# PSUM banks dealt out anew before the last blocks of the attention pass: two for value products and two for projections in place of one and three

## The chip, the cores and the metric

One NeuronCore of a Trainium2 chip runs the whole kernel. The metric is device time in microseconds (us), lower is better. Five engines work from queues of their own: TensorE (PE in the profile; its weight loads are PEld), VectorE (DVE), ScalarE (ACT), GpSimd (POOL) and SyncE (SP, which issues transfers). TensorE writes only to PSUM, which this kernel divides into eight banks; one bank holds a tile of 128 partitions by 512 fp32 values. ACT and DVE read the result out of a bank ("evict" it), and only then may TensorE start the next tile in the same bank.

## The reference

One encoder layer over x of 4096 tokens by 1024 features, with two groups of heads side by side, fp32 throughout. Only what matters here is kept:

```python
hn = rms_norm(x, norm_w)
proj = hn @ w_in                      # 1024 x 3856, cut into the parts below
qk_a, v_a, o_a, z_a, g_a, q_b, k_b, v_b, z_b = split(proj)
# group A: mLSTM, 4 heads x 128, both directions, short convolution on q and k
qk_a = silu(centred_depthwise_conv(qk_a, conv_w, conv_b))
h = sigmoid(o_a) * (mlstm(q_a, k_a, v_a, gates) + backwards mlstm)
y_a = head_norm(h) * silu(z_a)
# group B: attention in blocks of 128 queries over 384 keys, |i-j| <= 128,
# 8 query heads, 2 key/value heads of 64, a bias by distance, a sink per head
p = exp(scores + bias - m);  denom = sum(p) + exp(sink - m)
y_b = (p @ v_b) / denom * silu(z_b)
return rms_norm(x + concat(y_a, y_b) @ w_out, final_norm_w)
```

## The kernel before

The kernel runs four stages. **Pass 1** normalises x, keeps its transposed high and low parts in DRAM (`xT_d`), and computes the attention of group B. **Pass 2** goes backwards over the tokens and computes values, keys and queries of group A, their convolution and the chunks' outer products. **Pass 3** runs the mLSTM forwards. The **tail** does the gate of group B, the output projection and the last norm. An fp32 product is made of three reduced-precision products (low by high, high by low, high by high), so a projection of 1024 features is 8 x 3 = 24 matmuls into one bank. TensorE's order is written by hand (`manual_schedule` for PE); the order of ACT, DVE and POOL is laid out ahead by a planner, which goes by its own estimate of times and by priority, earlier program lines first. Each engine runs its queue strictly in that order.

**PSUM.** `c.psum(nb)` closes the pool of banks in use and opens a new one; `c.ps(tag, ...)` takes a tile of the pool that is open, from the banks of its tag. With `reuse_waits="tile"`, a tile of a new pool waits only for the tiles of the old one that lay in the same bank. Banks are dealt to tags in the order in which the tags are first used. The pool that is opened at the start, `{"pj": 3, "a": 2, "b": 2, "c": 1}`, therefore lies so: pj in banks 0 to 2, c in 3, a in 4 and 5, b in 6 and 7. It serves pass 1 and pass 2; the next call is at L1016, at the head of pass 3 (`{"pj": 2, "n": 2, "c": 1, "y": 1}`, pj in banks 0 and 1), the last at the head of the tail (`{"pj": 8}`).

**Pass 1** works on slots: slot `sl` is one block of 128 queries (n = sl // 2) for one of the two key heads. Its tiles are

- `sp`, tag a: scores of one of four heads (L359, two matmuls), evicted by DVE at L362;
- `tp`, tag b: four transposes for one of three key blocks (L387), evicted by ACT at L389 and DVE at L390;
- `op`, tag c: the value product, two matmuls for each of the three key blocks (L401), evicted by ACT at L413 and then by DVE at L414 (`AB`);
- tag pj: the projections, `qp` (L524, 24 matmuls; evicted at L534 by ACT, L538 by DVE), `kp` (L460; L471 and L472 by ACT, L476 and L477 by DVE), `vp` (L492 and L493; L498 by ACT, L499 by DVE) and `v2p` (L574; L579 by ACT).

A slot's pieces, written `p = [Sc(0), O(0), Sc(1), T(0), O(1), Sc(2), T(1), O(2), Sc(3), T(2)]`, take the scores of two slots ahead, the transposes of its own and the value product of the slot before. `interleave` spreads these pieces evenly over the matmuls of the projections. The main loop runs 13 rounds of four slots; after it the last twelve slots (52 to 63) are interleaved with the last projections, in this order: four `qp` of block 14, `kp` 15, `vp` 30 and 31, four `qp` of block 15, and `v2p` 31 to 28. At the seam, the first piece that runs is the scores of slot 54, and then three matmuls of the first `qp`, the value product of slot 51, four more of `qp`, and the scores of slot 54's second head. In the program before, the last tiles in their banks at that point are: `kp` 14 in bank 0, `vp` 29 in bank 1, `vp` 28 in bank 2, `op` of slot 50 in bank 3, the scores of slot 53 in 4 and 5.

**Pass 2** goes over eight blocks b = 7 to 0 of 512 tokens. For each block but the first it makes four value tiles `v2p` (L829, 24 matmuls each, evicted by ACT at L835), two at a time: three matmuls of the one, three of the other, through eight k. Then come the keys `up` m = 4 to 7 and the queries m = 0 and 1 (L856, 24 matmuls each, evicted by ACT at L860, after which ACT starts the convolution at L872), one after another. `last_two` then makes m = 2 and m = 3, again three matmuls of the one and three of the other (in block 7 each tile is in two parts, and only the second parts alternate). All of these are tag pj:

```python
vu = [vproj(4 * b + i) for i in pair]          # pairs (3, 2), (1, 0)
for k in range(KT):
    for u in vu[0][3 * k:3 * k + 3] + vu[1][3 * k:3 * k + 3]:
        u()
...
for k in range(KT):                            # last_two
    out += p2[-1][k] + p3[-1][k]
```

In between stand, in tags a and b, the transposes of the keys (`ktp`, L904) and the outer products (`kv`, L158 to L160, evicted by ACT at L934 and DVE at L935). Nothing in pass 2 uses tag c.

**Pass 3** begins with the projections `op` and `zp` of tokens 0 to 127 and `op` of the next (L1148, evicted from L1155 on by ACT).

Of the kernel before, what the change touches and what calls it, by code (L numbers as in the profile page):

```python
# [131 lines left out]
def interleave(fill, pieces):  # L132
    cum = np.cumsum([0.0] + [getattr(f, "cost", 1.0) for f in fill])
    done = 0
    for i, p in enumerate(pieces):
        while done < len(fill) and cum[done + 1] <= cum[-1] * i / len(pieces) + 1e-6:
            fill[done]()
            done += 1
        p()
    for f in fill[done:]:  # L140
        f()
# [26 lines left out]
def pass1(c):  # L168
    nc, tc, A = c.nc, c.tc, c.A
    NB = 16  # L170
    with ExitStack() as es:
# [437 lines left out]
        for b in range(NB - 3):  # L609
# [10 lines left out]
                f2.insert(p, u)  # L620
            interleave(f2, A2)
        c.x7 = XT
        pieces = []
        for sl in range(4 * (NB - 3), 4 * NB):
            pieces += slot(sl)
# [844 lines left out]
def body(nc, tc, A):  # L1470
    with ExitStack() as es:
        c = setup(nc, tc, A, es)
        c.w3, c.w4, c.XR = [], [], {}

        def next_weights(i):
            c.w3.append(wgroup(c, (1536, 2048, 2560)[i], f"w3_{i}"))

        c.next_weights = next_weights
        with tc.manual_schedule(engines={mybir.EngineType.PE}):
            pass1(c)  # L1480
            pass2(c)
            pass3(c)
            c.psum_es.close()
# [43 lines left out]
```

## Time and profile before

| | |
|---|---|
| Median of 3 runs | 2218.36 us (2217.43 to 2219.31) |
| The profiled execution | 2218.53 us, of which 2216.8 us span |
| Pass 1, to the last value projection | 0 to 608 us |
| of it the last twelve slots | 499 to 608 us |
| Pass 2 | 608 to 1192 us |
| Pass 3 and tail | 1192 to 2217 us |

In the rows shown further on, a group's row has the engine, line, operation and tiles (out<-in), the count, busy time and the idle time just before it with what ended it. A row of the waits has what waited, for what, the total in us, how often, and the longest. A row of the timeline has the start and the length in us, engine, line, operation, tiles and count, and in brackets the idle time before. The windows' rows have, for a stretch of time, its length, the busy time of each engine with its count of instructions, then TensorE's granted clock as a share of full speed (PEclk), the DMA engines' share and GB/s. A matmul of 512 columns lasts 0.39 us but the next starts some 0.23 us after it, so rows overlap by about 0.16 us.

### The profile page before, as it was taken

To read this page: it belongs to the slowest core of one execution; us is meant where nothing else is said; L and a number is where in the kernel's file an instruction comes from. 1 tells how busy PE (TensorE), PEld (TensorE's weight loads), DVE (VectorE), ACT (ScalarE), POOL (GpSimd) and SP (SyncE) were. 2 spreads that over 40 slices of the span, in tenths; PEclk is the share of its full clock that TensorE was granted. 3 is DMA by queue.
4 is the path that set the end of the run, shared out by engine and by line. 5 is a ranking of instruction groups with operands and counts; after the bars stand their busy time and mean duration, and the time that the engine had idled before them with its cause. 6 is when DMAs were issued, how large, how long until landed. Compare 5 with 4: busy or idle time off the path is not lost.

```text
span 2216.8 us, 35208 instructions
## 1 busy us (share of the span) xinstructions
PE 2165.7 (98%) x12226; PEld 1880.3 (85%) x12226; DVE 1407.0 (63%) x3090; ACT 1075.4 (49%) x2711; POOL 607.3 (27%) x1059
## 2 busy tenths in 40 slices
PE   7999999999999999999999999999999999999998
PEld 6899999998797888888887888888888888888886
DVE  5687777787865566556667555455554443877776
ACT  5788888887643343334445434444443321333323
POOL 2565665662121211121112111111111111112222
PEclk9999999999999999999999999999999999999999
DMA  7653555432233452344267976777785898667774
GB/s 235 184 158 114 170 142 125 156 109 76 86 95 114 158 163 80 116 158 154 80 196 217 302 226 209 240 239 229 215 251 176 306 355 290 183 185 185 190 193 140
DMA packets 249126, 398.98 MB, mean 180 GB/s; under 512 B 21971, under 2 KB 128467, under 8 KB 248948
## 3 DMA queue, kind: packets, MB, share of 16 engines
q1 hardware_dynamic: 220628, 303.57, 45.1%
q0 software_dynamic: 28176, 92.96, 13.1%
q8 instruction: 96, 1.57, 0.3%
q14 instruction: 82, 0.67, 0.1%
q10 hardware_dynamic: 144, 0.20, 0.0%
HBM read 275.99 MB, written 120.67 MB: 179 GB/s over the span
## 4 chain that ended last, share of the span: by engine, by line
PE 77%; DMA 9%; issue 5%; DVE 4%; ACT 3%; POOL 2%; SPq 1%; POOLq 0%; DVEq 0%; ACTq 0%
PE up L856 15%; PE op L1148 7%; PE zp L1148 7%; PE qp L524 7%; PE v2p L829 7%; DMA xr<-x 5%; PE op L401 4%; PE tp L387 3%; PE sp L359 3%; PE zbp L158 3%; PE zbp L160 3%; PE zbp L159 3%; PE num L1101 2%; PE num L1100 2%; PE o L1314 2%
## 5 line engine op out<-in xcount | busy, mean ns | idle before, releaser
L856 PE MATMUL up<-xb,w 128*128 128x512 f32 x1344 | 338.4, 396 | 0.0
L1314 PE MATMUL o<-wo,yo 128*128 128x512 f32 (+1 forms) x1356 | 312.3, 392 | 0.0
L1314 PEld LDWEIGHTS o<-wo,yo 128*128 128x128 f32 x1356 | 253.2, 188 | 59.2
L856 PEld LDWEIGHTS up<-xb,w 128*128 128x128 f32 x1344 | 243.7, 188 | 47.2
L874 DVE SCALAR_TENSOR_TENSOR qk<-U,cw,qk 128x512 f32<-128x512 f32 x256 | 190.1, 755 | 93.4 <-ACT qk L872 89.6
L524 PE MATMUL qp<-xT,wqb 128*128 128x256 f32 x1536 | 246.2, 291 | 0.0
L524 PEld LDWEIGHTS qp<-xT,wqb 128*128 128x128 f32 x1536 | 217.9, 193 | 9.8 <-issue 1.7
L1148 PE MATMUL op<-w,xs 128*128 128x512 f32 x720 | 203.9, 411 | 2.4 <-ACT E L1069 2.4
L1148 PE MATMUL zp<-w,xs 128*128 128x512 f32 x720 | 188.6, 402 | 2.4 <-DVE z L1157 2.4
L829 PE MATMUL v2p<-w,xb 128*128 128x512 f32 x672 | 157.8, 395 | 0.6 <-DMA xb<-xT_d 0.5
L1148 PEld LDWEIGHTS zp<-w,xs 128*128 128x128 f32 x720 | 131.2, 189 | 29.4 <-DVE z L1157 2.8
L829 PEld LDWEIGHTS v2p<-w,xb 128*128 128x128 f32 x672 | 126.0, 188 | 31.1 <-DMA xb<-xT_d 1.5
L1115 ACT ACTIVATE hs<-num,r 128x128 f32<-128x128 f32 x128 | 46.9, 367 | 216.4 <-DVE r L1112 173.3
L362 DVE CUSTOM_DVE_ANT_0 s<-sp,G 128x320 f32<-128x320 f32 (+1 forms) x256 | 122.8, 480 | 41.5 <-PE sp L359 38.5
L1148 PEld LDWEIGHTS op<-w,xs 128*128 128x128 f32 x720 | 127.8, 191 | 24.0 <-ACT E L1069 2.8
L371 ACT ACTIVATE s<-s,st 128x320 f32<-128x320 f32 (+1 forms) x256 | 139.8, 549 | 12.4 <-DVE st L369 12.0
L390 DVE TENSOR_TENSOR pt<-tp,pt 128x512 fp32r<-128x512 f32 x188 | 129.3, 688 | 25.3 <-ACT pt L389 24.2
L389 ACT CAST pt<-tp 128x512 fp32r<-128x512 f32 x188 | 109.9, 586 | 58.1 <-PE tp L387 54.9
L401 PE MATMUL op<-pt,v 128*128 128x512 f32 x376 | 121.5, 404 | 13.2 <-DVE ab L414 13.2
L359 PE MATMUL sp<-kk,q 128*128 128x320 f32 (+2 forms) x512 | 118.8, 313 | 0.0
L387 PE MATMUL tp<-ident,s 128*128 128x128 f32 x752 | 113.8, 274 | 0.2 <-DVE pt L390 0.2
L158 PE MATMUL zbp<-xc,w 128*128 128x512 f32 x256 | 101.5, 397 | 0.0
(273 smaller groups left out, 4443.3 us busy)
## 6 DMA issues: line engine op xcount, KB each, us to landing
xc<-xT_d SPq DMA_DIRECT2D x64, 512.0 KB, 8.0
xs<-xT_d SPq DMA_DIRECT2D x120, 256.0 KB, 6.4
xT_d<-xT POOLq DMA_DIRECT2D x104, 256.0 KB, 5.5
xb<-xT_d SPq DMA_DIRECT2D x48, 514.0 KB, 10.7
E<-m_d SPq DMA_DIRECT2D x64, 256.0 KB, 4.7
W<-w_d SPq DMA_DIRECT2D x64, 256.0 KB, 5.8
y<-y_d SPq DMA_DIRECT2D x32, 512.0 KB, 3.5
out<-xr POOLq DMA_DIRECT2D x31, 512.0 KB, 4.5
```

The source lines that it names most:

```text
L158: nc.tensor.matmul(out, wl, xh, start=first, stop=False)
L359: nc.tensor.matmul(sp[:, lo:hi], qt, kk[:, kv, z, col - 128 + lo:col - 128 + hi], start=(z == 0), stop=(z == 1))
L371: nc.scalar.activation(ps[g][:, kept(g)], ps[g][:, kept(g)], AF.Exp, bias=ng[:, g:g + 1], accum_out=rs[:, g:g + 1])
L387: nc.tensor.transpose(tp[:, g * 128:(g + 1) * 128], ps[g][:, j * 128:(j + 1) * 128], c.ident)
L390: nc.vector.tensor_sub(pt[:, 1, :], tp, f32(pt[:, 0, :]))
L401: nc.tensor.matmul(op, vt, pt[:, z, :], start=(i == 0 and z == 0), stop=(i == len(js) - 1 and z == 1))
L524: nc.tensor.matmul(qp, wq[k // 2][:, k % 2, w, m * 128:m * 128 + 128], x[k], start=(k == 0 and j == 0), stop=(k == KT - 1 and j == 2))
L829: nc.tensor.matmul(vp, a, wv[k // 2][:, k % 2, m, :], start=(k == 0 and j == 0), stop=(k == KT - 1 and j == 2))
L856: nc.tensor.matmul(up[:, 0:hi - lo], w[k // 2][:, k % 2, a, cs], x, start=(k == 0 and j == 0), stop=(k == KT - 1 and j == 2))
L874: nc.vector.scalar_tensor_tensor(acc, U[:, t:t + 512], cw[:, cm, t:t + 1], acc, ALU.mult, ALU.add)
L1148: nc.tensor.matmul(P[nm], XS[n](a, k), w[:, m, :], start=(k == 0 and j == 0), stop=(k == KT - 1 and j == 2))
L1314: nc.tensor.matmul(p, a[:, z, k, :], w[k // 2][:, k % 2, m, lo:hi], start=k == 0 and z == 1, stop=k == 3 and z == 0 and m == 0)
```

## The change

Before the last twelve slots, one call opens a new pool of banks:

```diff
             interleave(f2, A2)
         c.x7 = XT
+        c.psum({"pj": 2, "a": 2, "b": 2, "c": 2})
         pieces = []
         for sl in range(4 * (NB - 3), 4 * NB):
             pieces += slot(sl)
```

From there on tag c has two banks and tag pj two in place of three; a and b keep two each. No instruction is added or taken away, and TensorE's order stays. By the order of first use (scores, projection, value product, transposes) the new pool lies so: a in banks 0 and 1, pj in 2 and 3, c in 4 and 5, b in 6 and 7. The pool stays open until the call at L1016, so it serves the whole of pass 2 too.

## The prediction

> **What bounds the kernel now.** I read the page's head, then TensorE's waits from 470 to 612 us, the stage that the change names, and then the windows and the timeline of pass 2, because the new pool stays open there.
>
> ```profile
> span 2216.8 us, 35208 instructions
> PE 2165.7 (98%) x12226; PEld 1880.3 (85%) x12226; DVE 1407.0 (63%) x3090; ACT 1075.4 (49%) x2711; POOL 607.3 (27%) x1059
> ...
> PE op L401 <- DVE ab L414: 9.2, 7, 3.5
> ...
> 700.00:1190.00 490.00, 489.00 (x2327) 404.63 (x2327) 309.96 (x479) 202.94 (x370) 96.34 (x216) 1.00 0.42 134
> ```
>
> The reader is to see three things. TensorE is busy for 98% of the span, so the kernel is as long as TensorE's order plus its stalls. In the last slots the value product waits for its one bank, 9.2 us in 7 waits: that is what the change can win there. In pass 2 (last row) TensorE is busy 489 of 490 us: a stall made there lengthens the kernel by its own size.
>
> **Part one, the second bank of the value product.** The timeline of TensorE, and then of DVE:
>
> ```profile
> 498.92 0.50 PE L359 MATMUL sp<-kk,q 128*128 128x320 f32 x2
> 499.25 0.51 PE L524 MATMUL qp<-xT,wqb 128*128 128x256 f32 x3
> 503.28 0.89 PE L401 MATMUL op<-pt,v 128*128 128x512 f32 x2 [3.51 <-DVE ab L414]
> 504.83 0.73 PE L359 MATMUL sp<-kk,q 128*128 128x320 f32 x2
> ...
> 513.89 0.74 PE L401 MATMUL op<-pt,v 128*128 128x512 f32 x2 [0.61 <-DVE ab L414]
> ...
> 516.50 0.62 PE L401 MATMUL op<-pt,v 128*128 128x512 f32 x2
> ...
> 536.30 0.34 PE L492 MATMUL vp<-wkv,xT 128*128 128x288 f32 x1
> ...
> 565.17 0.60 PE L387 MATMUL tp<-ident,s 128*128 128x128 f32 x4
> ...
> 568.41 0.74 PE L401 MATMUL op<-pt,v 128*128 128x512 f32 x2 [1.65 <-DVE ab L414]
> ...
> 583.46 0.60 PE L387 MATMUL tp<-ident,s 128*128 128x128 f32 x4
> ...
> 585.32 0.73 PE L401 MATMUL op<-pt,v 128*128 128x512 f32 x2 [0.33 <-DVE ab L414]
> ...
> 600.56 0.74 PE L401 MATMUL op<-pt,v 128*128 128x512 f32 x2 [1.07 <-DVE ab L414]
> ```
>
> ```profile
> 502.55 0.68 DVE L414 TENSOR_TENSOR ab<-op,ab 64x512 f32<-64x512 f32 x1
> ...
> 503.95 0.29 DVE L499 TENSOR_TENSOR vg<-vp,vg 128x144 f32<-128x144 f32 x1
> ...
> 536.22 0.43 DVE L477 TENSOR_TENSOR kk<-kp,kk 64x256 fp32r<-64x256 f32 x1
> ...
> 564.19 0.69 DVE L390 TENSOR_TENSOR pt<-tp,pt 128x512 fp32r<-128x512 f32 x1
> ...
> 582.11 0.69 DVE L390 TENSOR_TENSOR pt<-tp,pt 128x512 fp32r<-128x512 f32 x1
> ```
>
> *The price of a wait.* L414 ends at 503.23 and the value product starts at 503.28: 0.05 us from eviction to start. Behind a stall the pair of matmuls takes 0.74 us, without one 0.62: 0.11 us more, rounded. So a stall costs the missing time plus 0.16 us.
>
> *The first stall (3.51 us) mostly stays.* In the new pool the value product of slot 51 gets bank 4, long free. But after slot 54's first score (498.92), three matmuls of the projection, that product and four matmuls more comes slot 54's second score, now in bank 1, where `vp` 29 lies, and L499 reads that until 504.24. TensorE would reach this score at about 500.6, stand until 504.29, and be there 0.5 us earlier than now (504.83). That is all: **0.5**.
>
> *The six others* are 9.2 - 3.5 = 5.7 us, with the restarts (6 x 0.11) 6.4. They vanish wholly if evictions move up with TensorE. *What is late next:* `vp` 31, with two projection banks, needs the bank of `kp` 15, which L477 leaves at 536.65; it starts at 536.30 now, so it loses 0.35 + 0.16 = 0.5. Upper end of the gain: 0.5 + 6.4 - 0.5 = **6.4**. Lower end: DVE keeps its present times. Then the transposes at 565.17 cannot start before 564.93 (L390 ends at 564.88), so of all that was won before only 0.24 is left; the stall at 568.41 gives 1.65 + 0.11; the transposes at 583.46 wait for L390's end at 582.80 and cut what is won to 0.6; the last two stalls give 0.33 + 1.07 + 0.22: **2.2**. DVE does have idle time, so part of its work moves up; neither end is nearer, and I take the middle, **4.3 us won**.
>
> **Part two, pass 2 with two projection banks in place of three.** One seam between blocks, block 6 to 5, TensorE and then ACT, which stands for the other five:
>
> ```profile
> 743.13 22.46 PE L829 MATMUL v2p<-w,xb 128*128 128x512 f32 x96
> 765.43 1.33 PE L856 MATMUL up<-xb,w 128*128 128x512 f32 x5
> ```
>
> ```profile
> 742.63 0.59 ACT L860 COPY U<-up 128x512 f32<-128x512 f32 x1
> 743.25 0.82 ACT L872 ACTIVATE qk<-U,cb,cw 128x512 f32<-128x512 f32 x1
> 743.97 0.57 ACT L860 COPY U<-up 128x512 f32<-128x512 f32 x1
> ...
> 753.78 0.59 ACT L835 COPY v<-v2p 128x512 f32<-128x512 f32 x1 [2.77 <-PE v2p L829]
> ...
> 764.93 0.59 ACT L835 COPY v<-v2p 128x512 f32<-128x512 f32 x1 [3.94 <-PE v2p L829]
> ```
>
> The 96 matmuls start 0.232 us apart ((765.43 - 743.13) / 96). Where tiles are made two at a time, both banks are full at the end, and with only two banks the next tile must wait for a copy out of PSUM that takes 0.59 us; the third bank hid this.
>
> - First value tile: wants to start at 743.13, its bank (m = 2) is free at 743.22: 0.09 + 0.16 = 0.25.
> - Its partner: 3 matmuls later, 743.83, now 744.08. Its bank (m = 3) is free only at 744.54, since ACT does the convolution's L872 between the two copies: 0.46 + 0.16 = 0.62.
> - First tile of the second pair: 743.13 + 48 x 0.232 = 754.27, bank free at 754.37: 0.10 + 0.16 = 0.26. Its partner has the same distance, but is already 0.26 late: nothing.
> - First key tile: 765.43, bank free at 765.52: 0.25.
>
> That is 0.87 at each of six such seams and 0.51 in each of seven blocks: 5.2 + 3.6 = 8.8. Nothing hides it, as TensorE has no idle time there. Block 7 to 6 is different:
>
> ```profile
> 660.12 1.11 PE L856 MATMUL up<-xT,w 128*128 128x256 f32 x8
> 667.51 8.59 PE L829 MATMUL v2p<-w,xb 128*128 128x512 f32 x36
> 676.57 14.56 PE L829 MATMUL v2p<-w,xb 128*128 128x512 f32 x60 [0.48 <-DMA xb<-xT_d]
> ```
>
> ```profile
> 660.59 0.36 ACT L860 COPY U<-up 128x258 f32<-128x258 f32 x1
> ...
> 667.65 0.70 ACT L860 COPY U<-up 128x256 f32<-128x256 f32 x2
> ```
>
> The second part of m = 3 starts with the third matmul from 660.12 on, at 660.36, and its bank is free at 660.95: 0.59 + 0.16 = 0.75. The first value tile, 667.51, waits for the first of two copies, until 668.0: 0.5 + 0.16 = 0.66, of which the wait for a transfer at 676.57 takes back up to 0.48. I take 1.2. Part two: **10.0 us lost**. Bounds: without the restarts (0.11 each, 28 of them) 7; and if another order of ACT sets an operation of L872's 0.82 us before one copy in each block, 4 more, 14.
>
> **Part three, the head of pass 3.** Its first tile lies in bank 0, now last used by m = 3, afterwards by `kv`:
>
> ```profile
> 1192.33 5.84 PE L1148 MATMUL op<-w,xb 128*128 128x512 f32 x24 [1.44 <-ACT U L860]
> ...
> 1204.40 5.87 PE L1148 MATMUL op<-w,xb 128*128 128x512 f32 x24 [0.67 <-ACT o L1155]
> ```
>
> The 1.44 go, but the third tile waits for ACT's L1155 in any case, 6 us after the first tile's end (1192.33 + 5.84 to 1204.40): the wait of 0.67 grows instead. I take **0**, at best 1.5 won.
>
> **Sum.** The profiled execution took 2218.53 us, 0.17 over the median of 2218.36. 2218.5 - 4.3 + 10.0 = **2224.2 us**, slower by 0.26%. Bounds of the sum: 7 - 6.4 - 1.5 = -0.9 to 14 - 2.2 = +11.8, so 2217.6 to 2230.3.
>
> **The rivals.**
>
> *A wash.* Evictions move up with TensorE, all of part one comes to 6.4: 2222.1 us, inside 0.2%. For it: DVE is busy 63% of the span, so it has room to follow. Against: two tiles of transposes stand within 0.3 and 0.7 us of their own evictions.
>
> *Not slower.* The planner, seeing other banks, puts L499 ahead of DVE's backlog, and the first stall goes too. The rows:
>
> ```profile
> 498.21 1.84 DVE L559 SCALAR_TENSOR_TENSOR w<-w2s,nw,w 128x512 fp32r<-128x512 f32 x1
> ...
> 500.42 0.28 ACT L498 COPY vg<-vp 128x144 f32<-128x144 f32 x1
> ...
> 503.20:506.80 3.60, 3.52 (x16) 3.38 (x16) 2.24 (x8) 1.54 (x6) 1.31 (x5) 0.57 0.28 100
> 514.40:518.00 3.60, 3.60 (x29) 3.47 (x29) 2.54 (x9) 3.18 (x12) 0.20 (x1) 1.00 0.38 135
> 558.60:562.00 3.40, 3.40 (x25) 3.22 (x26) 2.69 (x8) 2.04 (x6) 2.54 (x3) 1.00 0.08 30
> ```
>
> It decides where L499 ends before 500.6, for which L498 on ACT must come earlier too. Price: 3.5 - 0.5 = 3.0, and the slow clock behind that stall (0.57 for 3.6 us, 1.5 us lost). With 6.4 and 1.5 at the head of pass 3, 12.4 won against 10.0: 2216.1 us; with part two at its lower end 2213.
> Against: L498 needs the last matmul of `vp` 29, which stands beside the score at 498.92, and L559 has begun by then.
>
> *The wrong bank.* Slot 54's first score, not its second, gets `vp` 29's bank: TensorE stands from 498.9 to 504.3 ahead of the value product, which then starts at about 505.1 in place of 503.28. Instead of 0.5 won, 1.8 lost: 2226.5 us.
>
> *Many small stalls slow the clock.* If each of seven seams brought the 1.5 us of a slow clock, 10.5 more: 2234.7 us. Against: behind the stalls of 0.61 and 1.58 us the granted clock was 1.00 (last two rows); only the one of 3.51 was followed by 0.57. The Trainium skill, page "TensorE: Matmul & The Clock Gate", section "A second HAM failure mode: psum-queue depth-cycling", tells of a kernel that cycled through PSUM banks and idled briefly so often that the clock gate swung between half and full rate; by that rule this rival would be the forecast, and the trace does not agree so far.
>
> **Chances.** The forecast, 2222.9 to 2230: 0.45. A wash: 0.33. Not slower: 0.12, of which 0.07 beyond 0.2%. The wrong bank: 0.06. The slow clock: 0.04. A measurement of this kernel can tell about 0.2% (4.4 us) from no change, so: slower 0.45 + 0.06 + 0.04 = 0.55; same 0.33 + 0.05 = 0.38; faster 0.07. The range, 2217 to 2229, leaves out most of "not slower" (0.09), the slow clock (0.04) and the end of the forecast (0.05).
>
> **What would show it.** Right: in the waits up to 612 us the value product is gone, `sp` waits some 3.6 us for L499 near 504, and `tp`, `sp` or `vp` have small waits; in pass 2 `v2p` and `up` wait for L860 and L835, some 28 times, 0.1 to 0.6 us each, about 7 us in all. Wrong: no waits at L829 in pass 2; or the copies of m = 3 ahead of L872, which leaves the partner's 0.62 out; or a clock under 1.00 in pass 2.

## The result, and the profile after

| | before | after |
|---|---|---|
| Median (range), 20 runs each | 2217.18 us (2213.71 to 2220.97) | 2222.81 us (2218.2 to 2226.04) |
| Ratio after to before | | 1.0024, 95% interval 1.0018 to 1.0031 |
| The profiled execution | 2218.53 us | 2218.20 us |

The change makes the kernel slower by 5.3 us (0.0024 x 2217; by its interval 4.0 to 6.9, and the two medians lie 5.6 apart); 5.7 had been forecast. Two things must be known to read the rest. The code after the new call stands one line lower, so L829 of before is L830 of after. And the profiled execution of after is its fastest, 4.6 us under its median, so the two spans are alike and say nothing. The places where the kernels differ are found by the start of one and the same instruction in both timelines:

| us, TensorE, from the start of one to the start of the other | before | after | difference |
|---|---|---|---|
| Last slots: slot 54's first score (L359) to the first `up` of pass 2 | 109.54 | 106.52 | -3.02 |
| Pass 2: from there to the second `op` tile of pass 3 | 595.94 | 604.29 | +8.35 |
| of it block 7's keys to the first value tile of block 6 | 59.05 | 60.05 | +1.00 |
| of it the four value tiles of block 6 | 23.46 | 22.81 | -0.65 |
| of it one block, mean of four (keys of block 5 to keys of block 1) | 74.40 | 75.78 | +1.38 |
| Pass 3: the second `op` tile to the first `zbp` at its end | 506.29 | 503.75 | -2.54 |

By the start of pass 3's second tile, after is 8.35 - 3.02 = 5.33 us late, which is what the median of many runs says too. That this one execution makes up 2.5 of it in pass 3 goes with the clock: before's had two stretches at half clock there, from 1223.91 and from 1694.95 us on, some 1.7 us each, and after's none (last section).

First the head of the page of after, and TensorE's waits in the last slots (what waited, for what, the total in us, how often, the longest):

```profile
span 2216.5 us, 35220 instructions
PE 2168.7 (98%) x12226; PEld 1875.7 (85%) x12226; DVE 1411.1 (64%) x3090; ACT 1076.2 (49%) x2711; POOL 609.5 (27%) x1059
```

The 12 instructions more handle semaphores; the operations of the engines are the same in number as before.

```profile
PE sp L359 <- DVE vg L499: 3.2, 1, 3.2
PE tp L387 <- DVE pt L390: 1.4, 2, 0.8
PE gp L682 <- DVE st L369: 1.3, 1, 1.3
PE sp L359 <- DVE st L362: 0.9, 1, 0.9
PE vp L492 <- DVE kk L477: 0.5, 1, 0.5
```

Before, the value product (L401) waited 9.2 us here in 7 waits. It waits no more: the second bank does what it is for. In its place stand five rows with 7.3 us. The largest is the wait of a score for L499, which is slot 54's second score at the place that was forecast. The timeline of TensorE there:

```profile
498.06 0.50 PE L359 MATMUL sp<-kk,q 128*128 128x320 f32 x2
...
498.74 0.63 PE L401 MATMUL op<-pt,v 128*128 128x512 f32 x2
499.21 0.64 PE L524 MATMUL qp<-xT,wqb 128*128 128x256 f32 x4
503.02 0.56 PE L359 MATMUL sp<-kk,q 128*128 128x320 f32 x2 [3.17 <-DVE vg L499]
```

The value product starts at 498.74 without a wait; then the second score stands 3.17 us, because bank 1, which the scores now have, still holds `vp` 29.

Now the seam of blocks 6 and 5 in pass 2, TensorE and then ACT:

```profile
738.72 1.09 PE L857 MATMUL up<-xb,w 128*128 128x512 f32 x4
739.80 0.97 PE L830 MATMUL v2p<-w,xb 128*128 128x512 f32 x3
741.12 22.13 PE L830 MATMUL v2p<-w,xb 128*128 128x512 f32 x93 [0.35 <-ACT U L861]
763.22 6.98 PE L857 MATMUL up<-xb,w 128*128 128x512 f32 x29
```

```profile
739.16 0.59 ACT L861 COPY U<-up 128x512 f32<-128x512 f32 x1
739.78 0.81 ACT L873 ACTIVATE qk<-U,cb,cw 128x512 f32<-128x512 f32 x1
740.50 0.56 ACT L861 COPY U<-up 128x512 f32<-128x512 f32 x1
```

The first value tile starts at 739.80, 0.05 us behind the end of the first copy (739.16 + 0.59 = 739.75). Its partner starts at 741.12, 0.06 behind the end of the second (740.50 + 0.56), and between the copies ACT does the convolution's L873. Both waits, and their price, are those of the prediction. The row of 93 matmuls holds the second pair's wait: at 0.232 us a start, 93 take 21.58, and 22.13 less the 0.16 of overlap is 21.97, so 0.39 is lost, 0.11 on the restart and 0.28 where 0.26 was worked out. Such a wait is not listed at all, since a matmul is shown as busy for 0.16 us past the next start; that is why the view of waits tells of less than is lost:

```profile
PE v2p L830 <- ACT U L861: 2.1, 6, 0.4
PE ktp L905 <- DVE qk L878: 1.0, 1, 1.0
PE up L857 <- ACT v L836: 0.2, 1, 0.2
```

Six partners' waits are there, 2.1 us by the view. What is lost must be read from the distance of equal instructions: 1.38 us in each block.

### The profile page after: what moved, and what is told of

Same layout as the page of the kernel before. It is cut to its first block, busy times and chain, and to the rows that moved or that the text cites. A ratio compares the mean times of both kernels' runs of the same rounds, so it can differ in the third digit from the quotient of the medians.

```text
span 2216.5 us, 35220 instructions
## 1 busy us (share of the span) xinstructions
PE 2168.7 (98%) x12226; PEld 1875.7 (85%) x12226; DVE 1411.1 (64%) x3090; ACT 1076.2 (49%) x2711; POOL 609.5 (27%) x1059
## 5 line engine op out<-in xcount | busy, mean ns | idle before, releaser
L830 PE MATMUL v2p<-w,xb 128*128 128x512 f32 x672 | 161.3, 397 | 2.2 <-ACT U L861 2.1
L830 PEld LDWEIGHTS v2p<-w,xb 128*128 128x128 f32 x672 | 124.2, 188 | 39.0 <-ACT U L861 7.5
L362 DVE CUSTOM_DVE_ANT_0 s<-sp,G 128x320 f32<-128x320 f32 (+1 forms) x256 | 122.7, 480 | 37.4 <-PE sp L359 33.9
L390 DVE TENSOR_TENSOR pt<-tp,pt 128x512 fp32r<-128x512 f32 x188 | 129.3, 688 | 22.3 <-ACT pt L389 20.7
L401 PE MATMUL op<-pt,v 128*128 128x512 f32 x376 | 120.7, 402 | 3.0 <-DVE ab L414 3.0
L359 PE MATMUL sp<-kk,q 128*128 128x320 f32 (+2 forms) x512 | 119.1, 314 | 4.1 <-DVE vg L499 3.2
```

The source lines that it names most:

```text
L359: nc.tensor.matmul(sp[:, lo:hi], qt, kk[:, kv, z, col - 128 + lo:col - 128 + hi], start=(z == 0), stop=(z == 1))
L362: nc.vector.tensor_tensor_reduce(out=s[:, lo:hi], in0=sp[:, lo:hi], in1=bias[0][:, kv * 2 + m, lo - 64 * half:hi - 64 * half], op0=ALU.add ...
L390: nc.vector.tensor_sub(pt[:, 1, :], tp, f32(pt[:, 0, :]))
L401: nc.tensor.matmul(op, vt, pt[:, z, :], start=(i == 0 and z == 0), stop=(i == len(js) - 1 and z == 1))
L830: nc.tensor.matmul(vp, a, wv[k // 2][:, k % 2, m, :], start=(k == 0 and j == 0), stop=(k == KT - 1 and j == 2))
```

## The experiments

Three questions stand behind them. Does the loss come from the two projection banks in pass 2 alone? Is the partner's wait there due to L873 between the copies? And is the first stall of the last slots due to the bank that slot 54's second score was dealt, or to what DVE is doing then? Each was timed against the kernel before on the same chip; the ratios are to before.

**Three banks again in pass 2.** A second call at the head of pass 2 brings the old dealing back, so that only the last slots differ from before:

```diff
         wk = es.enter_context(tc.tile_pool(name="p2", bufs=1, reuse_waits="tile"))
+        c.psum({"pj": 3, "a": 2, "b": 2, "c": 1})
```

> The changed kernel, but at the head of pass 2 the old counts come back (pj 3, a 2, b 2, c 1). If the loss is the two projection banks in pass 2 (some 1.4 us in each block, as in the trace after: from -3.3 us at block 5 to +3.5 us at block 0 against before), pass 2 takes as long as before it did, and only the gain of the last twelve slots stays, 3 us: about 2214 us, 0.9985 of the kernel before, and the waits for L861 and L836 at the value tiles are gone. If the loss comes from another order of ACT and DVE after the new pool, or sits in pass 3, it stays at about 2222 us.

Measured: 2215.63 us (2209.75 to 2222.24, 12 runs), ratio 0.9993 (0.9983 to 1.0003). The interval lies wholly under that of after (1.0018 to 1.0031), so the loss is gone. That the second bank for value products alone makes the kernel faster is not shown, though 3 us had been expected: the interval reaches from 3.8 us less than before to 0.7 more. The profile: the last slots take 107.60 us (1.94 less than before), pass 2 takes 596.69 (before 595.94, after 604.29), one block 74.40, as before to the hundredth. TensorE's waits in pass 2, from 700 us on, are down to one row, and `v2p` is not among them:

```profile
PE ktp L906 <- DVE qk L879: 1.1, 1, 1.1
```

Another order of ACT or DVE is not the cause either: from block 6 on, ACT, DVE and POOL do the same operations in the same order in before and in after.

**Two banks in pass 2 alone.** The kernel before, with the last slots as they were and the new dealing from the head of pass 2 on:

```diff
         wk = es.enter_context(tc.tile_pool(name="p2", bufs=1, reuse_waits="tile"))
+        c.psum({"pj": 2, "a": 2, "b": 2, "c": 2})
```

> The kernel before, and only at the head of pass 2 a new pool with pj 2, a 2, b 2, c 2; the last slots keep their one bank for value products. If two projection banks in pass 2 cost 1.38 us in each of six blocks and 1.0 us in the first, less what the head of pass 3 returns, the kernel takes 8 to 9 us more than before: about 2226 us, 1.004. The stalls of the value product in the last slots stay at 9.2 us. If the loss comes from the last slots' new pool, it stays at 2217 us.

Measured: 2226.14 us (2224.44 to 2228.45, 5 runs), ratio 1.0039 (1.0027 to 1.0051). Pass 2 takes 604.53 us, 8.59 more than before, and the last slots 110.54 (before 109.54). Its waits, the last slots and pass 2 together, show both halves at once:

```profile
PE op L401 <- DVE ab L414: 8.8, 6, 3.5
...
PE v2p L830 <- ACT U L861: 2.1, 6, 0.4
```

The value product waits as before, and `v2p` as in after. So the change is a sum of two parts that do not need each other.

**The two copies back to back.** In pass 2 of after, what follows m = 2's copy (L873 and on) is recorded behind m = 3's copy. `behind`, a helper of the kernel, lets the planner place operations only after a given one:

```diff
-                nc.scalar.copy(U[:, lo:hi], up[:, 0:hi - lo])
+                cp = nc.scalar.copy(U[:, lo:hi], up[:, 0:hi - lo])
                 if hi != parts[-1][1]:
                     return
+                if b and m == 2:
+                    LATE[b] = lambda: rest(U)
+                elif b and m == 3:
+                    with behind(c, cp):
+                        LATE.pop(b)()
+                        rest(U)
+                else:
+                    rest(U)
+
+            def rest(U):
```

> The changed kernel, but in last_two (blocks 7 to 1) ACT's convolution of m = 2 is queued behind the copy of m = 3 out of its bank. If the second value tile's 0.62 us in each of six seams comes from that convolution step standing between the two copies, the copy of m = 3 ends 0.6 us earlier and this wait goes: 3 to 4 us less than the changed kernel, each block 0.6 us shorter (1.40 to 0.8 us over the kernel before), about 2219 us. If the wait has another cause, each block keeps its 1.40 us and the time stays at 2222 us.

Measured: 2220.02 us (2218.06 to 2223.33, 11 runs), ratio 1.0008 (0.9999 to 1.0017): less than after, the intervals do not meet. One block takes 75.17 us, 0.61 less than in after, which is the partner's 0.62. ACT now does both copies in a row and the convolutions after them:

```profile
741.12 1.28 ACT L862 COPY U<-up 128x512 f32<-128x512 f32 x2
742.29 1.52 ACT L884 ACTIVATE qk<-U,cb,cw 128x512 f32<-128x512 f32 x2
```

What is left, 75.17 - 74.40 = 0.77, is the other three waits of a block, worked out at 0.25 + 0.26 + 0.25 = 0.76.

**Another bank for the second score.** In after, the two first pieces change places, so that the value product is the first to touch a bank and the banks are dealt otherwise:

```diff
             pieces += slot(sl)
+        pieces[0:2] = pieces[1::-1]
```

> The changed kernel with the first two pieces after the new pool exchanged: the value product of slot 51 before the first score of slot 54. By the order of first use the value products then get banks 0 and 1, so nobody needs the bank of value/gate tile 29 for the next 10 us, and the scores get banks 4 and 5, which held scores. If the 3.2 us stall of the score for L499 is that bank, it goes, and with it the slow clock behind it (1.5 us): 4 to 5 us less than the changed kernel, about 2218 us, 1.0005 of the kernel before. If DVE's backlog holds TensorE there in any case, through the next score or transposes, the stall moves to another tile and the time stays at 2222 us.

Measured: 2222.55 us (2220.65 to 2225.46, 9 runs), ratio 1.0021 (1.0012 to 1.0031): no gain over after. Counted from the first of the two exchanged pieces, the last slots took 107.11 us (after 106.52). TensorE's waits there, and two rows of its timeline:

```profile
PE sp L359 <- DVE st L362: 3.0, 2, 2.5
PE tp L387 <- DVE pt L390: 2.7, 3, 1.0
```

```profile
502.53 0.63 PE L387 MATMUL tp<-ident,s 128*128 128x128 f32 x4 [1.01 <-DVE pt L390]
...
511.32 0.58 PE L359 MATMUL sp<-kk,q 128*128 128x320 f32 x2 [2.52 <-DVE st L362]
```

The wait for L499 is gone, and 1.01 and 2.52 us are lost a little later, at other tiles that DVE evicts. So the bank only says which tile stands. What made DVE late for the longer of the two is seen in ACT's and DVE's timeline of the same run:

```profile
508.57 0.72 ACT L558 ACTIVATE w<-w2s,nw 128x512 fp32r<-128x512 f32 x1 [3.17 <-DMA w2s<-w_in]
509.32 1.54 DVE L559 SCALAR_TENSOR_TENSOR w<-w2s,nw,w 128x512 fp32r<-128x512 f32 x1 [2.53 <-ACT w L558]
510.78 0.48 DVE L362 CUSTOM_DVE_ANT_0 s<-sp,G 128x320 f32<-128x320 f32 x1
```

DVE was not busy. L558 and L559 prepare weights of pass 2 whose transfer had not landed; ACT stood 3.17 us for it and DVE 2.53 us for ACT, and the eviction L362, which TensorE needed, stood behind L559 in DVE's queue. In after, at the time of the wait for L499, the same L559 is ahead of the evictions and takes long. DVE's timeline there, and POOL's:

```profile
497.34 1.84 DVE L559 SCALAR_TENSOR_TENSOR w<-w2s,nw,w 128x512 fp32r<-128x512 f32 x1
499.11 1.65 DVE L369 SCALAR_TENSOR_TENSOR st<-st,nsink 128x4 f32<-128x4 f32 x1
500.68 0.68 DVE L390 TENSOR_TENSOR pt<-tp,pt 128x512 fp32r<-128x512 f32 x1
501.28 0.67 DVE L414 TENSOR_TENSOR ab<-op,ab 64x512 f32<-64x512 f32 x1
...
502.68 0.29 DVE L499 TENSOR_TENSOR vg<-vp,vg 128x144 f32<-128x144 f32 x1
```

```profile
497.33 1.30 POOL L556 TENSOR_TENSOR w<-w2s,w 128x512 fp32r<-128x512 f32 x1
...
499.65 1.08 POOL L265 TENSOR_TENSOR xT<-xraw,xT 128x512 fp32r<-128x512 f32 x1
```

These weights are first used by `v2p` at 561.02 us, some 64 us later. L559 takes 1.84 us beside POOL here (0.75 at 503.73 us), and L369, an operation on 128 x 4 values, takes 1.65 us.

**Pass 2's weights held back.** In after, the planner may place the first load and preparation of those weights only behind the last softmax operation of ACT (`LAST["act"]`) that was recorded by the ninth piece:

```diff
-        hooks = [(40, lambda: w2_load(0, 0)), (80, lambda: gate1(c, wk)), (100, lambda: gate2(c, wk)),
+        def w2_held():
+            with behind(c, LAST["hold"]):
+                w2_load(0, 0)
+
+        hooks = [(9, lambda: LAST.__setitem__("hold", LAST["act"])), (40, w2_held), (80, lambda: gate1(c, wk)), (100, lambda: gate2(c, wk)),
```

> The changed kernel, with the preparation of pass 2's first weights (L555 to L559) held on ACT until the softmax of slot 54 in place of beginning in front of the last slots. If DVE's backlog at 498 to 504 us is these weights and what they share with POOL, the 3.2 us stall of the score for L499 shrinks to under 1 us and its slow clock goes with it: 3 to 5 us less than the changed kernel, about 2219 us, with perhaps a wait of the value projections at 561 us for weights that now come later. If the backlog is the attention's own work, the stall stays at 3 us and the time at 2222 us.

Measured: 2223.42 us (2216.69 to 2225.02, 11 runs), ratio 1.0020 (1.0011 to 1.0029). The stall is gone, but not the time. In the last slots, its waits and two rows of DVE's timeline:

```profile
PE tp L387 <- DVE pt L390: 2.6, 2, 2.2
PE gp L686 <- DVE st L369: 1.3, 1, 1.3
PE vp L492 <- DVE kk L477: 0.9, 1, 0.9
PE sp L359 <- DVE vg L499: 0.3, 1, 0.3
```

```profile
499.92 0.15 DVE L369 SCALAR_TENSOR_TENSOR st<-st,nsink 128x4 f32<-128x4 f32 x1
...
500.59 0.29 DVE L499 TENSOR_TENSOR vg<-vp,vg 128x144 f32<-128x144 f32 x1
```

The score's wait falls from 3.2 to 0.3 us, L369 takes 0.15 us, and the last slots take 102.98 us, 3.5 less than in after; 1.7 of it is the stretch at half clock that follows the stall in after and is absent here. But the stretch from the second `op` tile to the end of pass 3 took 508.50 us (after 503.75), with waits at the head of pass 3 that after's profile does not have and a granted clock under 1.00 there (waits, then windows: start and end, length, busy time and count of PE, PEld, DVE, ACT and POOL, clock, DMA share, GB/s):

```profile
PE op L1153 <- ACT o L1160: 2.3, 1, 2.3
PE num L1105 <- DVE hs L1121: 1.6, 1, 1.6
PE op L1153 <- DMA xs<-xT_d: 1.0, 1, 1.0
```

```profile
1206.00:1212.00 6.00, 4.74 (x14) 3.81 (x15) 0.69 (x1) 1.68 (x4) 0.00 (x0) 0.72 0.52 148
1230.00:1236.00 6.00, 5.65 (x25) 4.87 (x26) 4.61 (x11) 0.89 (x3) 0.00 (x0) 0.72 1.09 363
```

Half clock makes up most of the difference: three stretches of it, from 1207.05, 1230.94 and 1698.57 us on, against none in after's profile, which is that of its fastest execution. The waits need not come from holding the weights: `num` waits 1.6 us also in the kernel with two banks in pass 2 alone.

To see whether that was chance, the same kernel was run once more:

> The kernel with the weights held once more, for a second profile and further times, since its last slots were 3.5 us shorter than the changed kernel's while its time was not. If its head of pass 3 always takes about 2 us more, the time is 2222 to 2223 us again. If that was a matter of which stalls happened to be followed by half clock in the executions seen, the time is 2219 to 2220 us and the profile shows another number of half-clock stretches there.

Measured: 2221.72 us (2215.93 to 2228.21, 11 runs), ratio 1.0023 (1.0011 to 1.0035); last slots 102.53 us, and again 508.93 from the second `op` tile on, with as many stretches at half clock. In 22 runs the median does not fall, and in both profiles what is won in the last slots is lost again behind the second `op` tile.

**The same, with pass 2 mended.** Three more kernels hold the weights back: with three banks in pass 2 (the call of the first experiment), on the kernel before, and with the two copies back to back:

> The changed kernel with the weights held and the old counts of banks at the head of pass 2. If the three causes add up (3 us won in the last slots, 3 to 4 more at the seam, nothing lost in pass 2), TensorE reaches pass 3 6 us earlier than in the kernel before; the head of pass 3, where the DMA engines are busy all the time, gives some of it back, as it did in the run with three banks alone: 2212 to 2214 us, 0.998. If all of it is given back there: 2217 us.

> The kernel before, only with the weights held. If the first of the seven stalls (3.5 us) is DVE's backlog from these weights and not the count of banks, it goes here with one bank for value products too: 3 to 5 us less than before, about 2213 us. If the second bank is needed for it, the stall stays and the time is 2217 us.

> The changed kernel with the weights held and with ACT's copies first in last_two; pass 2 keeps two projection banks. If the two edits add up (3.5 us less in the last slots, 3.7 less in pass 2), TensorE reaches pass 3 about 2 us earlier than in the kernel before, and the time is 2214 to 2217 us, 0.999. If the head of pass 3 takes back what comes early, as it seemed to with the weights held alone, 2218 to 2220 us, 1.001.

Measured, with the two parts that differ:

| | median (range, runs) | ratio (95%) | last slots | pass 2 | pass 3 from its second `op` |
|---|---|---|---|---|---|
| after, held, three banks in pass 2 | 2213.71 (2208.65 to 2219.61, 12) | 0.9982 (0.9973 to 0.9991) | 102.35 | 597.80 | 506.29 |
| before, held | 2214.65 (2213.37 to 2218.58, 11) | 0.9989 (0.9980 to 0.9998) | 103.77 | 596.89 | 506.98 |
| after, held, copies first | 2215.11 (2210.99 to 2218.61, 11) | 0.9993 (0.9984 to 1.0002) | 105.02 | 600.94 | 505.34 |

All three take less time than the same kernel without held weights (2215.63, the kernel before, 2220.02), but only for the kernel before is that shown; in the other two pairs the intervals overlap. The first two are faster than before, by 0.2 and 0.1%. The kernel before wins 5.8 us in its last slots (109.54 to 103.77) without a second bank at all, 1.7 of it again a stretch at half clock; its waits there:

```profile
PE op L401 <- DVE ab L414: 3.6, 4, 1.2
```

The value product's 9.2 us in 7 waits have become 3.6 in 4. So 5.6 of the 9.2 us that the second bank was to win came from the early work on these weights. Whether the second bank adds something to that can't be told from these runs: 0.9982 and 0.9989 have intervals that overlap.

**Four banks in pass 2.** The exchange of pieces above, and four projection banks with none for tag c, which pass 2 does not use:

```diff
         wk = es.enter_context(tc.tile_pool(name="p2", bufs=1, reuse_waits="tile"))
+        c.psum({"pj": 4, "a": 2, "b": 2})
```

> The exchange of the run before, and a pool with pj 4, a 2, b 2 at the head of pass 2. If both causes hold and add up: 3 us from the last slots, 4.5 us from the seam, nothing lost in pass 2; a fourth projection bank gives nothing more, since with three there was no wait of size. About 2210 us, 0.9965 of the kernel before. If the causes overlap, about 2214 us; if a fourth bank does help in pass 2, under 2208 us.

Measured: 2218.64 us (2214.14 to 2223.73, 11 runs), ratio 1.0008 (0.9997 to 1.0019). Pass 2 takes 596.91 us, with three banks 596.69: a fourth wins nothing. The total is not told apart from that of three banks (0.9983 to 1.0003). About 2210 us had been expected: the 4.5 us at the seam did not come, as the run with the exchange alone had shown, and pass 3 took 508.94 us from its second `op` tile, with three stretches at half clock.

## Why the prediction was right

**Part two, the loss in pass 2, is shown.** It goes with the third bank (first experiment) and comes with its loss alone (second). One block costs 1.38 us, worked out as 0.87 + 0.51 = 1.38, and its terms are confirmed apart: 0.61 of it is the partner's wait behind the convolution (0.62), 0.77 the rest (0.76). In all 10.0 was forecast and 8.35 found. Most of the difference lies where block 7 goes over to block 6: forecast 1.2 and 0.51 for block 6's own waits, found 1.00 - 0.65 = 0.35. The keys' side lost what was forecast; but the transfer that block 6's value tiles waited for in before is no longer late when TensorE arrives 1.0 us later. I allowed up to 0.48 for that, the wait as listed, while the four tiles took 23.46 us there and 96 matmuls at 0.232 take 22.27: 1.19 us were to be had back. Two tiles of the transfer were late there, for the matmuls at 676.57 and at 678.35 us, and each cost a restart too; the view lists 0.48 for the first and nothing for the second.

**Part one, the gain in the last slots, has the right form and a smaller size:** 3.0 us for 4.3, within its bounds of 2.2 and 6.4. From first to second score TensorE needed 504.83 - 498.92 = 5.91 us before and 503.02 - 498.06 = 4.96 after, so the first stall gave 0.95 (forecast 0.5). The rest gave 3.02 - 0.95 = 2.07, where 6.4 were upper end. New waits took the other: 1.4 for L390 (foreseen, "what is late next"), 0.5 for L477 (foreseen, 0.35 + 0.16), 0.9 for L362 (named only as possible), and 1.3 by `gp`, a matmul of the gates (not foreseen). The view puts that one down to L369; what `gp` reads was written by the operation just ahead of it, until 590.15 us, and `gp` starts at 590.30. DVE moved less of its work up than the middle that I took. The planner also laid DVE's queue out in another order in the last slots, so the 3.0 us are those of the new call as a whole, not of the banks alone.

**Part three, the head of pass 3,** came out in kind: the wait of 1.44 for a copy of pass 2 is gone, and the wait for the output gate's eviction has grown from 0.7 to 2.0 us, together 0.1 won where I took 0:

```profile
PE op L1149 <- ACT o L1156: 2.0, 1, 2.0
```

**The rivals.** A wash (2222.1 us) lies close to the time measured, 2222.81, which even falls just under the forecast's own lower bound of 2222.9, since the sum started from an execution 1.3 us over the median of the 20 runs of before. But its reason does not hold: it wanted 6.4 us from the last slots. The time fits better than the terms deserve: the gain was forecast 1.3 too large and the loss 1.6 too large, and that the two errors nearly cancel is luck. Not slower: it wanted L499 ahead of DVE's backlog, and L499 stood behind it as before. The wrong bank: it was the second score, not the first. Many small stalls that slow the clock: this window of after holds four blocks of pass 2 with their waits, and the clock is 1.00:

```profile
750.00:1050.00 300.00, 298.60 (x1396) 241.96 (x1396) 177.36 (x271) 114.24 (x207) 56.92 (x128) 1.00 0.38 126
```

The Trainium skill's rule on such cycling through PSUM banks (page "TensorE: Matmul & The Clock Gate", section "A second HAM failure mode: psum-queue depth-cycling") therefore did not come to bear: idle times of at most 0.6 us, some four in 75 us, left the clock as it was.

**What stays open.** Why the weights held back in the kernel after do not show in its median. In both its profiles the half clock behind the second `op` tile takes what the last slots won; how much half clock a usual execution of after has there is not known, since only its fastest was profiled. Nor was it taken apart what makes ACT, DVE and the transfer late at the head of pass 3. Part of what comes early there is given back in waits alone: the kernel with held weights and three banks in pass 2 starts its second `op` tile earliest of all, at 1199.47 us, and took 506.29 us from there without any half clock, where after, 9.4 us later and also without, took 503.75.

## What to carry to other kernels

A pool of PSUM banks that is opened for one stage serves all that follows until the next call, so price a new dealing in every stage that it reaches: here a gain of 3.0 us in 109 was paid for with 1.38 us in each block of a stage in which TensorE had no idle time. Tiles that are made two at a time wanted a third bank here; an evicting engine that does both copies before anything else won back 0.61 of the 1.38 us. And where a stall names a bank, look at what the evicting engine did in the time before: moving a preparation that is not needed for another 64 us out of its queue won 5.8 us in the last slots, where the second bank won 3.0; in the time of the whole kernel the two are not told apart.

## What the runs showed of the hardware

**A stall of some us can be followed by half clock, in whole stretches of 3.4 us, and not always.** Behind the stall of 3.17 us in after:

```profile
504.00:507.40 3.40, 3.40 (x16) 3.20 (x15) 1.85 (x6) 0.62 (x2) 0.35 (x1) 0.50 0.71 224
```

At half clock a stretch of 3.4 us does the work of 1.7, so it costs 1.7 us where TensorE is busy throughout. One and the same wait is punished in one execution and not in another: late in pass 3, `zp` waits 2.0 to 2.7 us for DVE's L1157 in all twelve profiles; in nine a stretch at half clock goes with it, in three none. First before, then after:

```profile
1693.47 0.96 PE L1148 MATMUL zp<-w,xs 128*128 128x512 f32 x3 [2.38 <-DVE z L1157]
```

```profile
1697.00 0.96 PE L1149 MATMUL zp<-w,xs 128*128 128x512 f32 x3 [2.39 <-DVE z L1158]
```

The traces show what decides. In each profile all stretches at half clock begin a whole number of times 3.4133 us apart, from the first to the last of the kernel: in before those from 503.70, 1223.91 and 1694.95 us on are 211 and 138 such steps apart. Cut by this grid, what counts is how long TensorE is idle within one step. Two steps of before, then one of after:

```profile
1691.54:1694.95 3.41, 1.48 (x7) 1.26 (x8) 1.85 (x6) 0.00 (x0) 0.10 (x1) 1.00 0.00 0
1694.95:1698.36 3.41, 3.41 (x13) 2.95 (x12) 0.00 (x0) 0.00 (x0) 0.00 (x0) 0.50 0.00 0
```

```profile
1695.20:1698.61 3.41, 1.61 (x9) 1.39 (x10) 1.74 (x5) 0.00 (x0) 0.00 (x0) 1.00 0.00 0
```

In before 1.93 us of the wait lie in one step, and the next step is at half clock. In after the wait falls across two steps, with 1.80 us idle in the fuller one, and the clock stays. Over all twelve profiles, from 95 to 2195 us: each of the 22 steps at full clock with over 1.95 us idle is followed by half clock, none of the 7303 with under 1.53 us, and 8 of the 25 between. So in this kernel a stall of under 1.5 us costs only itself, and for one of 2 us it depends on how it falls on the grid.

At the head of pass 3, between 1200 and 1240 us, there is one such stretch in before, none in after and two in each profile of the kernel with held weights. From the second `op` tile to the end of pass 3, the stretch near 1695 us counted too, the four profiles with three stretches took 508.5 to 508.9 us, the four with two 505.3 to 506.3, those with one 505.1 and 507.0, and those with none 503.8 and 506.3: three stand apart, the others overlap. This is probably also why executions of one kernel lie some 8 us apart: among the 20 runs of after, the four with a mean granted clock of 0.992 have a median of 2224.64 us, the three with 0.995 one of 2218.66.

The Trainium skill, page "TensorE: Matmul & The Clock Gate", section "The HAM clock gate (the "warmup" mystery)", tells of a window of 3413 ns that is free-running and does not reset when a kernel starts. The trace agrees in the length of the stretches and in the fixed grid on which they lie.

**A small operation of DVE can take ten times its time beside POOL.** L369, on 128 x 4 values, took 1.65 us in after, where POOL was at work on tiles of 128 x 512, and 0.15 us in the kernel with held weights, where POOL's operation had ended 0.08 us before. The rows of DVE stand above. All 64 of L369 in after fit: the 34 beside no operation of POOL took 0.14 to 0.17 us; the 17 that took over 0.3 us all lie beside an operation of POOL on 128 x 512 and end 0.01 to 0.03 us after it. The Trainium skill, page "SBUF — State Buffer", section "Who interferes with whom", says that DVE and GpSimd share a pair of ports under an exclusive lock; these ends agree with that, though no run here held POOL's operation back alone.
